# Moving part of an encoder layer's transfers from SyncE's queue to GpSimd's

## The chip, the cores and the metric

The kernel runs on one core of one Trainium2 chip. The metric is the device time of one execution in microseconds, lower is better; a time given for a kernel is the median of its runs. The core has TensorE (PE; weight loads are shown as PEld), VectorE (DVE), ScalarE (ACT), GpSimd (POOL) and SyncE (SP). Transfers are issued from an engine's queue: here SP's and, after the change, POOL's too. Each engine executes its own instructions in a fixed order, and an instruction that waits holds up those behind it.

## The reference

One layer of an encoder over 256 tokens of width 2048, in fp32:

```python
mod = silu(c) @ W_ada + b_ada            # 2048 x 12288: shift1, scale1, gate1, shift2, scale2, gate2
h = x * (1 + scale1) + shift1
x = layer_norm(alpha * x + gate1 * mixer(h))
h = x * (1 + scale2) + shift2
x = layer_norm(alpha * x + gate2 * peer(h))
```

mixer: one input projection (2048 x 11328), a bidirectional state-space scan with 32 heads in 2 chunks of 128 tokens (its decay rows are cumulative sums over time), a gated short convolution, group norms, and one output projection (4096 x 2048). peer: queries (2048 x 4096), two sets of 128 keys for each of 8 heads, the best 16 pairs, and gelu(h . u) times the gate times v over 16384 experts. All 16384 are computed here as dense products with expert_u and expert_v, with gates that are zero for those not chosen.

## The kernel before

**Weight tiles.** Nearly everything is a stream of weight tiles of 128 x 1024 fp32 (512 KB; w_inA's are 128 x 768). `wsplit` (L68 to L83) loads a tile into `raw`, lets ScalarE round it to fp32r (`hi`, L78) and VectorE subtract (`lo`, L81), and TensorE multiplies with both parts (`mm3`). `raw`, `hi` and `lo` have three buffers each. So SP may issue the next weight load when VectorE has finished `lo` of the tile three back.

**adaLN.** The six parts of `mod` are products of one vector with a 2048 x 2048 matrix each. They are made on VectorE: `ada_half` (L148 to L153) multiplies a 128 x 1024 tile of w_ada with the broadcast vector `scb` and sums along the row (L152). Parts 0 and 1 come in the front, 64 such tiles, loaded by `ada_load` (L281) into four buffers of 1 MB; parts 2, 3 and 4 beside the input and output projections, 96 tiles through two buffers `adaw` (`ada_step`, L163); part 5, 32 tiles, at the start of the expert_v stage through two quarters of the tile `big` (also L163). Those quarters take the last columns of expert_v later (L893).

**Stages, in order.** The front (w_inA, w_inB and the first adaLN parts: TensorE can use a row block d of h only when its two mod values are there); the rest of w_in beside the scan, which loads decay rows `bct` from DRAM (L529), written once as `acs_d` (L501); the output projection with `ax`, rows of x (L642); layer norm; the query projection with the keys `sk` (L710) and the residual written to `ax_d` (L692); expert_u, where the first 64 Gelu rows go to DRAM (`gel_d`, L841, from one buffer `ge`) and come back in the second half (`gb`, L849, two buffers); expert_v with part 5 of adaLN, whose result is written as `g2_d` in 4-byte pieces and read back broadcast as `g2b` (L914, L915); the last layer norm.

**What sets the order.** The program is written for a scheduler: it emits each engine's instructions in an order of its own, by the priorities given in the code (`high_priority(offset=...)`) and by its own estimate of when operands are ready. All 1245 transfers go out on SP's queue, in one such order.

## Time and profile before

| | |
|---|---|
| time, median of 3 runs | 2547.92 us (2544.36 to 2559.14) |
| profiled execution | 2552.61 us, of which the span is 2550.7 |
| TensorE busy | 2424.6 us (95%) |
| VectorE busy | 1862.2 us (73%) |
| ScalarE busy | 1381.3 us (54%) |
| GpSimd busy | 0.9 us |
| moved | 575.67 MB, mean 226 GB/s |
| granted TensorE clock, mean | 0.984 |

The busy time of an engine is the time in which one of its instructions executes; instructions that issue transfers are not counted. The shares are means over stages with different limits.

### The profile page before, as it was taken

Reading aid. Unit: us, or ns where it says so; the run is one execution under the profiler, and the core shown is the slowest. Engines: PE = TensorE matmul, PEld = TensorE weight load, DVE = VectorE, ACT = ScalarE, POOL = GpSimd, SP = SyncE. Lnnn points to the kernel's source line nnn. Section 1 sums busy time; section 2 is a strip of 40 time slices with the busy share of each in tenths; the row PEclk is TensorE's granted clock in tenths of the full one; section 3 lists DMA queues with packets and bytes.
Section 4 is the critical chain, followed back from the end, with each engine's and each line's share of the span. In section 5 each row is a group of like instructions: output and inputs, shape, how many; then the busy total and the mean of one; then the engine's idle time right before and its main releaser. Section 6 shows DMA issues by size and latency. Waiting matters only on the chain.

```text
span 2550.7 us, 44290 instructions
## 1 busy us (share of the span) xinstructions
PE 2424.6 (95%) x17122; PEld 2248.3 (88%) x17122; DVE 1862.2 (73%) x3255; ACT 1381.3 (54%) x2506; POOL 0.9 (0%) x7
## 2 busy tenths in 40 slices
PE   5889999999999899999999999999998999999997
PEld 5889888888899799999999999999886888888886
DVE  8788888989887799898888855555675555645545
ACT  3435476656444554499999944444443444544442
POOL 0000000000000000000000000000000000000000
PEclk9999999999999899999999999999999999999999
DMA  9886766778887565355666666666788655655554
GB/s 356 313 297 236 260 217 224 235 260 280 267 291 259 196 206 181 116 181 193 199 195 200 198 218 219 218 217 219 257 307 274 217 194 190 223 192 193 193 190 149
DMA packets 183252, 575.67 MB, mean 226 GB/s; under 512 B 22209, under 2 KB 44929, under 8 KB 182657
## 3 DMA queue, kind: packets, MB, share of 16 engines
q1 hardware_dynamic: 183042, 572.85, 67.3%
q8 instruction: 134, 2.20, 0.3%
q14 instruction: 76, 0.62, 0.1%
HBM read 560.10 MB, written 12.66 MB: 225 GB/s over the span
## 4 chain that ended last, share of the span: by engine, by line
PE 67%; DMA 15%; DVE 12%; ACT 3%; issue 2%; SPq 1%; DVEq 0%; ACTq 0%
PE ps_u L91 9%; PE ps_u L92 9%; PE ps_u L93 9%; PE ps_v L879 8%; PE ps_v L881 8%; PE ps_v L878 8%; DVE lo L81 5%; DMA adaw<-in_w_ada_dram 4%; DMA raw<-in_w_in_dram 3%; DMA big<-in_w_ada_dram 2%; ACT hi L78 2%; DVE adaw L152 2%; DMA raw<-in_w_inA_dram 2%; PE ps_q L93 2%; PE ps_q L92 2%
## 5 line engine op out<-in xcount | busy, mean ns | idle before, releaser
L81 DVE TENSOR_TENSOR lo<-raw,hi 128x1024 fp32r<-128x1024 f32 (+1 forms) x804 | 972.1, 1212 | 506.8 <-ACT hi L78 504.7
L78 ACT ACTIVATE hi<-raw 128x1024 fp32r<-128x1024 f32 (+1 forms) x804 | 843.6, 1051 | 884.6 <-PE ps_v L879 302.1
L91 PE MATMUL ps_u<-h2h,hi 128*128 128x256 f32 x2048 | 568.7, 278 | 0.0
L92 PE MATMUL ps_u<-h2l,hi 128*128 128x256 f32 x2048 | 568.1, 277 | 0.0
L93 PE MATMUL ps_u<-h2h,lo 128*128 128x256 f32 x2048 | 568.1, 277 | 0.0
L878 PE MATMUL ps_v<-hi,ah 128*128 128x512 f32 x992 | 390.1, 393 | 9.9 <-ACT hi L78 8.1
L879 PE MATMUL ps_v<-hi,al 128*128 128x512 f32 x992 | 390.7, 394 | 1.2 <-DVE al L120 1.2
L91 PEld LDWEIGHTS ps_u<-h2h,hi 128*128 128x128 f32 x2048 | 386.2, 189 | 0.0
L92 PEld LDWEIGHTS ps_u<-h2l,hi 128*128 128x128 f32 x2048 | 384.6, 188 | 0.0
L93 PEld LDWEIGHTS ps_u<-h2h,lo 128*128 128x128 f32 x2048 | 384.5, 188 | 0.0
L881 PE MATMUL ps_v<-lo,ah 128*128 128x512 f32 x992 | 268.9, 393 | 0.8 <-DVE lo L81 0.8
L878 PEld LDWEIGHTS ps_v<-hi,ah 128*128 128x128 f32 x992 | 187.5, 189 | 52.3 <-ACT hi L78 8.9
L879 PEld LDWEIGHTS ps_v<-hi,al 128*128 128x128 f32 x992 | 187.7, 189 | 43.0 <-DVE al L120 1.6
L91 PE MATMUL ps_in<-h2h,hi 128*128 128x256 f32 x768 | 222.3, 289 | 3.0 <-DVE mod L159 2.2
L881 PEld LDWEIGHTS ps_v<-lo,ah 128*128 128x128 f32 x992 | 186.8, 189 | 42.0 <-DVE lo L81 2.0
L93 PE MATMUL ps_in<-h2h,lo 128*128 128x256 f32 x768 | 217.6, 283 | 2.3 <-DVE lo L81 2.3
L152 DVE SCALAR_TENSOR_TENSOR adaw<-adaw,scb 128x1024 f32<-128x1024 f32 x160 | 193.1, 1219 | 35.3 <-DMA adaw<-in_w_ada_dram 35.0
L92 PE MATMUL ps_in<-h2l,hi 128*128 128x256 f32 x768 | 217.6, 283 | 0.0
L809 ACT ACTIVATE o<-eq,gT 128x128 fp32r<-128x128 f32 x512 | 161.4, 388 | 0.0
L91 PEld LDWEIGHTS ps_in<-h2h,hi 128*128 128x128 f32 x768 | 146.6, 191 | 9.0 <-issue 4.2
L93 PEld LDWEIGHTS ps_in<-h2h,lo 128*128 128x128 f32 x768 | 147.1, 191 | 4.6 <-DVE lo L81 2.9
L93 PE MATMUL ps_o<-y,lo 128*128 128x256 f32 x512 | 145.6, 284 | 5.0 <-DVE lo L81 4.9
(285 smaller groups left out, 3975.0 us busy)
## 6 DMA issues: line engine op xcount, KB each, us to landing
raw<-in_expert_u_dram SPq DMA_DIRECT2D x256, 512.0 KB, 4.5
raw<-in_expert_v_dram SPq DMA_DIRECT2D x248, 512.0 KB, 3.9
adaw<-in_w_ada_dram SPq DMA_DIRECT2D x160, 512.0 KB, 6.0
raw<-in_w_in_dram SPq DMA_DIRECT2D x110, 512.0 KB, 5.0
raw<-in_w_out_dram SPq DMA_DIRECT2D x64, 512.0 KB, 4.3
raw<-in_w_query_dram SPq DMA_DIRECT2D x64, 512.0 KB, 3.9
raw<-in_w_inB_dram SPq DMA_DIRECT2D x44, 512.0 KB, 4.4
big<-in_w_ada_dram SPq DMA_DIRECT2D x32, 512.0 KB, 5.6
```

Of the source, the lines that this page charges most:

```text
L78: A.activation(hi, raw, AF.Copy)
L81: V.tensor_tensor(lo, raw, hi.bitcast(F32), op=ALU.subtract)
L91: T.matmul(ps, wh, mh, start=start, stop=False)
L92: T.matmul(ps, wh, ml, start=False, stop=False)
L93: T.matmul(ps, wl, mh, start=False, stop=stop)
L152: V.scalar_tensor_tensor(w, w, 0.5, scb[:, cs], op0=ALU.mult, op1=ALU.mult, accum_out=macc[:, half, part % 2, d:d + 1])
L809: A.activation(o2[:, k], eq[:, i, 1].bitcast(F32), AF.Copy, scale=gT[:, k, t0 + i:t0 + i + 1])
L878: T.matmul(banks[tb][c], ah[:, ts], vh, start=start, stop=False)
L879: T.matmul(banks[tb][c], al[:, ts], vh, start=False, stop=False)
L881: T.matmul(banks[tb][c], ah[:, ts], vl, start=False, stop=stop)
```

## The change

`aside` is GpSimd's `dma_start`. It takes the place of SyncE's for adaLN's weights (but for the first step's in the front), the later blocks of x, the decay rows and their write, the residual's write, the keys, the staged Gelu rows both ways, and the vectors that are written and read back for the last stage. Weight tiles, the first inputs, the residual's reads, the last columns and the output stay on SyncE. No computation, buffer or priority is changed.

```diff
+    aside = nc.gpsimd.dma_start
...
     def ada_step(scb, ws, part, d):
         for half, w in enumerate(ws):
-            nc.sync.dma_start(w, I["w_ada"][part, d, :, half * 1024:(half + 1) * 1024])
+            aside(w, I["w_ada"][part, d, :, half * 1024:(half + 1) * 1024])
...
-                nc.sync.dma_start(wa[d, part][:, cs], I["w_ada"][part, d, :, cs])
+                (aside if d else nc.sync.dma_start)(wa[d, part][:, cs], I["w_ada"][part, d, :, cs])
...
-            nc.sync.dma_start(xt4[d // 4], I["xT"][:, d:d + 4])
+            aside(xt4[d // 4], I["xT"][:, d:d + 4])
...
-        nc.sync.dma_start(acs_d, acr.rearrange("h c t -> h (c t)"))
+        aside(acs_d, acr.rearrange("h c t -> h (c t)"))
...
-                nc.sync.dma_start(bct[:, dr].rearrange("p e c t -> p e (c t)"), bass.AP(
+                aside(bct[:, dr].rearrange("p e c t -> p e (c t)"), bass.AP(
...
-        nc.sync.dma_start(ax, I["xT"][:, d])
+        aside(ax, I["xT"][:, d])
...
-            nc.sync.dma_start(ax_d[:, :, d * P:(d + 1) * P].rearrange("b t d -> t b d"),
+            aside(ax_d[:, :, d * P:(d + 1) * P].rearrange("b t d -> t b d"),
...
-    nc.sync.dma_start(sk, I["sub_keys"])
+    aside(sk, I["sub_keys"])
...
-                nc.sync.dma_start(gel_d[e2], act_chunk(e2, wk, 1, step))
+                aside(gel_d[e2], act_chunk(e2, wk, 1, step))
...
-                nc.sync.dma_start(gb, gel_d[k])
+                aside(gb, gel_d[k])
...
-                nc.sync.dma_start(g2_d.rearrange("d p -> p d"), mod[:, 5])
-                nc.sync.dma_start(g2b, bass.AP(tensor=g2_d.tensor, offset=g2_d.offset, ap=[[0, P], [1, D]]))
+                aside(g2_d.rearrange("d p -> p d"), mod[:, 5])
+                aside(g2b, bass.AP(tensor=g2_d.tensor, offset=g2_d.offset, ap=[[0, P], [1, D]]))
```

The scheduler's order changes with it. Lines of the changed kernel are two higher than those of before from here on.

**The front.** SP's queue before, at its start, from the write of `sc_d` on (`adaw_189` and `adaw_192` are the two tiles of adaLN's second step, `raw` is a weight tile):

```order
L296 DMA sc_d<-scb 1x2048
L281 DMA adaw_189<-in_w_ada_dram 128x1024 x2
L281 DMA adaw_192<-in_w_ada_dram 128x1024 x2
L75 DMA raw<-in_w_inA_dram 128x768 x2
L281 DMA adaw_252<-in_w_ada_dram 128x1024 x2
L281 DMA adaw_255<-in_w_ada_dram 128x1024 x2
L75 DMA raw<-in_w_inA_dram 128x768 x2
L281 DMA adaw_315<-in_w_ada_dram 128x1024 x2
```

SP's queue of the changed kernel from the same row on:

```order
L298 DMA sc_d<-scb 1x2048
L77 DMA raw<-in_w_inA_dram 128x768 x9
L77 DMA raw<-in_w_inB_dram 128x1024
L77 DMA raw<-in_w_inA_dram 128x768
L77 DMA raw<-in_w_inB_dram 128x1024 x2
L77 DMA raw<-in_w_inA_dram 128x768
```

POOL's queue of the changed kernel, from its last fill on:

```order
L337 IOTA jp 128x128
L283 DMA adaw_189<-in_w_ada_dram 128x1024 x2
L283 DMA adaw_192<-in_w_ada_dram 128x1024 x2
L283 DMA adaw_252<-in_w_ada_dram 128x1024 x2
L283 DMA adaw_255<-in_w_ada_dram 128x1024 x2
L283 DMA adaw_315<-in_w_ada_dram 128x1024 x2
```

On SP the adaLN loads between the weight loads are gone, so that nine w_inA loads stand one behind the other; the same adaLN loads are the first transfers on POOL, in the order that they had.

**The output projection.** VectorE's order before, some way into the output projection (`adaw` is adaLN's multiplication, `lo` the split of a weight tile, `ln_a` and `ln_q` sums for the layer norm, `mod` the sums of adaLN):

```order
L152 SCALAR_TENSOR_TENSOR adaw,macc<-adaw,scb 128x1024
L192 TENSOR_TENSOR ln_a<-ln_a,rT 128x256
L197 TENSOR_TENSOR ln_q<-ln_q,ln_sq 128x256
L81 TENSOR_TENSOR lo<-raw,hi 128x1024
L158 TENSOR_TENSOR mod<-macc 128x1
L159 TENSOR_TENSOR mod<-mod,badaT 128x1
L81 TENSOR_TENSOR lo<-raw,hi 128x1024
L152 SCALAR_TENSOR_TENSOR adaw,macc<-adaw,scb 128x1024
L81 TENSOR_TENSOR lo<-raw,hi 128x1024
L152 SCALAR_TENSOR_TENSOR adaw,macc<-adaw,scb 128x1024
```

VectorE's order of the changed kernel at the same place:

```order
L160 TENSOR_TENSOR mod<-macc 128x1
L154 SCALAR_TENSOR_TENSOR adaw,macc<-adaw,scb 128x1024
L83 TENSOR_TENSOR lo<-raw,hi 128x1024
L194 TENSOR_TENSOR ln_a<-ln_a,rT 128x256
L199 TENSOR_TENSOR ln_q<-ln_q,ln_sq 128x256
L161 TENSOR_TENSOR mod<-mod,badaT 128x1
L154 SCALAR_TENSOR_TENSOR adaw,macc<-adaw,scb 128x1024
L83 TENSOR_TENSOR lo<-raw,hi 128x1024
L160 TENSOR_TENSOR mod<-macc 128x1
L154 SCALAR_TENSOR_TENSOR adaw,macc<-adaw,scb 128x1024
```

There is now a multiplication for each split. From the first tile of w_out on, the remaining multiplications stand among 20 splits or so, where before they were spread over 44.

**The expert_v stage.** VectorE's order before, in the middle of adaLN's last part (`big` is the multiplication, `al` a split of the activations):

```order
L152 SCALAR_TENSOR_TENSOR big_23146,macc<-big_23146 128x1024
L81 TENSOR_TENSOR lo<-raw,hi 128x1024
L152 SCALAR_TENSOR_TENSOR big_23146,macc<-big_23146 128x1024
L81 TENSOR_TENSOR lo<-raw,hi 128x1024 x2
L120 TENSOR_TENSOR al<-GA_12817,ah 128x512
L152 SCALAR_TENSOR_TENSOR big_23146,macc<-big_23146 128x1024
L81 TENSOR_TENSOR lo<-raw,hi 128x1024
L152 SCALAR_TENSOR_TENSOR big_23146,macc<-big_23146 128x1024
L81 TENSOR_TENSOR lo<-raw,hi 128x1024 x2
```

VectorE's order of the changed kernel at the same place:

```order
L154 SCALAR_TENSOR_TENSOR big_23146,macc<-big_23146 128x1024
L83 TENSOR_TENSOR lo<-raw,hi 128x1024
L154 SCALAR_TENSOR_TENSOR big_23146,macc<-big_23146 128x1024
L83 TENSOR_TENSOR lo<-raw,hi 128x1024
L154 SCALAR_TENSOR_TENSOR big_23146,macc<-big_23146 128x1024
L83 TENSOR_TENSOR lo<-raw,hi 128x1024
L122 TENSOR_TENSOR al<-GA_12817,ah 128x512
L154 SCALAR_TENSOR_TENSOR big_23146,macc<-big_23146 128x1024
L83 TENSOR_TENSOR lo<-raw,hi 128x1024
```

Two splits in a row no longer occur between multiplications: from the first of the 32 to the last there are 31 splits, where there were 43. The first load of the last columns on SP now follows the 37th weight tile of the stage.

## Rows read from the trace of the kernel before

**Rows 1.** The page of the profile: the span, and each engine's busy time.

```profile
span 2550.7 us, 44290 instructions
...
PE 2424.6 (95%) x17122; PEld 2248.3 (88%) x17122; DVE 1862.2 (73%) x3255; ACT 1381.3 (54%) x2506; POOL 0.9 (0%) x7
```

**Rows 2.** Busy us: length, PE, PEld, DVE, ACT, POOL, clock, DMA share, GB/s.

```profile
8.00:182.00 174.00, 139.53 (x1068) 133.86 (x1068) 142.50 (x247) 66.99 (x103) 0.00 (x0) 0.96 0.89 330
...
1825.00:1952.00 127.00, 126.22 (x549) 102.73 (x548) 95.23 (x118) 52.40 (x55) 0.00 (x0) 1.00 0.89 308
1955.00:1975.00 20.00, 11.92 (x45) 9.11 (x44) 6.26 (x6) 4.75 (x5) 0.00 (x0) 0.84 0.64 187
2000.00:2050.00 50.00, 50.00 (x220) 41.00 (x220) 25.10 (x24) 21.25 (x23) 0.00 (x0) 1.00 0.57 190
```

**Rows 3.** Waits between 50 and 212 us: who for whom, us, times, longest.

```profile
ACT hi L78 <- DMA raw<-in_w_inB_dram: 35.3, 22, 3.6
ACT hi L78 <- DMA raw<-in_w_inA_dram: 31.3, 8, 5.8
```

**Rows 4.** DMA issues, 50:212 and 2000:2400 us: count, KB each, median us to landing.

```profile
raw<-in_w_inA_dram SPq DMA_DIRECT2D x22, 384.0 KB, 7.1
...
raw<-in_expert_v_dram SPq DMA_DIRECT2D x146, 512.0 KB, 3.5
```

**Rows 5.** The split lo (L81) alone, in two stretches of the output projection.

```profile
651.00:796.00 145.00, 53.83 (x45) 0.98 0.87 290
800.00:846.00 46.00, 20.73 (x17) 1.00 0.67 213
```

**Rows 6.** Tile big, 1790 to 2060 us: adaLN's multiplication, its waits, loads' landing.

```profile
L152 DVE SCALAR_TENSOR_TENSOR big<-big x32: 1217/1225/1227, 1825.9 to 1951.6; 128x1024 f32<-128x1024 f32 x32
...
  DMA big<-in_w_ada_dram: 28.3, 29
...
DMA to landing us min/median/max: 4.3/5.6/14.6
```

**Rows 7.** The chain that ended last, 1870 to 1900 us: start, length, what.

```profile
1879.58 6.54 DMA big<-in_w_ada_dram
...
1888.54 0.33 SPq L75
...
1888.92 6.28 DMA big<-in_w_ada_dram
```

**Rows 8.** The first stretch with full DMA queues, columns as in rows 2.

```profile
20.00:30.00 10.00, 8.75 (x48) 8.29 (x49) 8.82 (x19) 4.82 (x8) 0.00 (x0) 1.00 1.03 409
```

**Rows 9.** DMA issues of the whole program, columns as in rows 4.

```profile
bct<-acs_d SPq DMA_DIRECT2D x32, 256.0 KB, 5.4
gel_d<-ge SPq DMA_DIRECT2D x64, 128.0 KB, 3.9
...
sk<-in_sub_keys_dram SPq DMA_DIRECT2D x1, 2048.0 KB, 13.0
...
ax<-ax_d SPq DMA_DIRECT2D x8, 256.0 KB, 3.0
```

**Rows 10.** The chain that ended last, 1950 to 1985 us.

```profile
1954.90 3.68 SPq L893
...
1958.68 12.12 DMA raw<-in_expert_v_dram
```

**Rows 11.** Instructions in order of time, 1300 to 1312 us, ScalarE, then SP.

```profile
1300.70 0.37 ACT L138 ACTIVATE ge<-ps_u 128x256 f32<-128x256 f32 x1
...
1304.13 0.39 ACT L818 ACTIVATE GA<-ps_g 128x124 f32<-128x124 f32 x1 [0.35 <-DVE GA L819]
...
1306.73 0.36 ACT L138 ACTIVATE ge<-ps_u 128x256 f32<-128x256 f32 x1
...
1301.45 0.33 SPq L841 DMA_DIRECT2D gel_d<-ge  x1
```

**Rows 12.** Who waited for the decay rows' load (L529), whole program.

```profile
  ACT Emat L536: 20.1, 13
```

More of the change, by code (lines that the diff above doesn't have):

```diff
@@ L861, in layer_kernel @@
         scb5 = big[:, 2:].rearrange("p a c -> p (a c)")
-        nc.sync.dma_start(scb5, bass.AP(tensor=sc_d.tensor, offset=sc_d.offset, ap=[[0, P], [1, D]]))
+        aside(scb5, bass.AP(tensor=sc_d.tensor, offset=sc_d.offset, ap=[[0, P], [1, D]]))
         banks = [[pv.tile([P, 512], F32, name="ps_v", tag="pm") for _ in range(4)] for _ in range(2)]
```

## The prediction

> **What bounds the kernel now.** I read the page first, then the busy time by stretches, then the waits and the chain in the stretches where TensorE is not full. TensorE is busy 95% of a span of 2550.7 us [rows 1], so about 126 us could be gained at most by moving transfers, and the question is where those lie. In the plain expert_v stretch TensorE is full and does 220 matmuls in 50 us; one weight tile of 1024 columns feeds 12 of them, so it eats a tile in 2.73 us [rows 2]. It is not full in three places that the change touches: the front (139.5 of 174 us), the output projection while adaLN steps run beside it, and the first 150 us of expert_v, which end in a hole of 8.1 us between 1955 and 1975 us [rows 2].
>
> In the front ScalarE's first half of each split (hi) waits for the weight tiles themselves, 31.3 and 35.3 us between 50 and 212 us [rows 3]. There a w_inA tile lands 7.1 us after its issue, where an undisturbed tile takes 3.5 us in the median [rows 4]: the adaLN tiles issued ahead of it on SP's queue, 2 MB per step, are in its way.
>
> Beside the output projection the same kind of tile needs longer too. From 651 to 796 us 45 splits (lo) pass in 145 us, which is 3.22 us each; from 800 to 846 us, with no adaLN step left, 17 pass in 46 us, 2.71 us each [rows 5]. In expert_v 32 adaLN steps run from 1825.9 to 1951.6 us, and VectorE waits for their loads 29 times, 28.3 us in all [rows 6]. The chain shows the loop: a load issued at 1879.58 lands 6.54 us later, VectorE multiplies (1.23 us) and splits the next weight tile, only then SP issues a weight load, and behind that the next adaLN load into the same buffer [rows 7]. Two buffers, 31 steps in 125.7 us: the loop is 8.1 us around. Its landing is 5.6 us in the median [rows 6], so 2.5 us of it are multiplication, the split and SP's turn.
>
> **The change part by part.** No work is added on TensorE, VectorE or ScalarE. 388 transfers leave SP's queue for POOL's, an engine that is busy 0.9 us of the span [rows 1], and this changes two things: who waits behind whom, and the order that the scheduler writes down for VectorE.
>
> *Front.* SP's order is now weight tiles alone; the adaLN steps load from POOL as their buffers come free. By 182 us 57 MB have moved (174 us at 330 GB/s), and the queue moves 409 GB/s when it is full [rows 2, 8]; so the bytes need 140 us. VectorE was busy 142.5 us there [rows 2], and the new order puts about 5 more adaLN multiplications of 1.22 us into the same number of splits: 149 us. That is the floor; the stretch as it is, 174 us, is the ceiling. Since VectorE takes turns in a fixed order and will wait for one stream or the other, I take the middle, 161: **13 us less**, between 25 and 0.
>
> *Output projection and expert_v.* Here the order matters. The written order now has the 32 multiplications of expert_v among 31 splits, one for one, where before there were 43 splits, and the last 20 in the output projection among some 21 splits of the 45. VectorE executes in order: a multiplication whose load is not there holds up the split behind it, and that holds up TensorE as soon as its three finished tiles are used. So a tile costs half a loop, R/2, as long as adaLN steps last, and 2.73 or 2.71 us after that. For expert_v: 31 x R/2 + 12 x 2.73 against 126 us; for the output projection 20 x R/2 + 24 x 2.71 against 145 us. Together 25.5 R + 98 - 271.
>
> What is R with POOL issuing? The multiplication stays, 1.23 us. The wait for the split and SP's turn goes; an issue is left, which I put at SP's 0.4 us. The landing is at best that of an undisturbed tile, 3.5 us [rows 4], and at worst today's 5.6 us [rows 6]; I take 4.6, because the load no longer stands behind a weight tile on one queue but still shares the engines with it. What POOL adds to a transfer no row shows, since POOL issues none before. Below, nothing. Above, I use the dearest difference that rows of equal size show for the handling of a transfer: 256 KB land in 5.4 us as small pieces (bct) and in 3.0 us as long rows (ax from ax_d), 2.4 us [rows 9]. adaLN's rows are 4 KB long, nearer to the lower end: 1.0 us. So R = 1.23 + 0.4 + 4.6 + 1.0 = 7.2 us, and the two stages come to 183.6 + 98 - 271 = **+10.6 us**: expert_v 18.3 slower, the output projection 8 faster. Bounds: R cannot pay below twice TensorE's pace, 5.46; above it is 1.63 + 5.6 + 2.4 = 9.6 us.
>
> The Trainium skill, "DMA: Bandwidth & Descriptors", section Latency and other measured facts, gives about 1 us to the first byte for a transfer issued from GpSimd and 0.6 us from SyncE; an estimate by that page would add 0.4 us in place of my 1.0, R would be 6.6, and the two stages would cost 15 us less than I say. No run so far shows it.
>
> *The hole at 1955.* SP issues g_d (8 KB in 4-byte pieces), then a load of the last columns that occupies it for 3.68 us, and the weight tile issued at 1958.68 lands 12.12 us later [rows 10]; g2b, which reads what g_d writes, comes next in SP's order. Both go to POOL, and nothing needs g2b before the end. **8 us less**; if the 4-byte pieces hold up the engines all the same, some 4.
>
> *Start of the query projection.* sk, 2 MB, lands in 13.0 us [rows 9], and some of the first weight tiles stand behind it on SP. **2 us less.**
>
> *At nothing, with a threshold.* gel_d, the write of each staged Gelu row, lands in 3.9 us on SP [rows 9], and there is one buffer: the next Gelu may not start before. One Gelu starts at 1300.70, its write is issued at 1301.45 and lands about 1305.35; the next Gelu starts at 1306.73 [rows 11]. So 1.4 us later costs nothing; with 1.0 us for POOL it is covered, by my upper value of 2.4 it is not: ScalarE would stand still 1.0 us, 64 times, with the next hi behind it, and what ScalarE idles there now (0.35 us per half) gives back some 0.4: 38 us. gb has two buffers and nothing waits for it.
>
> The decay rows (bct) stay behind adaLN loads on their queue as before; ScalarE waits 20.1 us for them now, 13 times [rows 12]. A microsecond more each costs 13 us if nothing covers it; I count nothing, as VectorE is the busier engine there. SP has no wait any more except for weight buffers, and for the first last-column load (L893 before), which stands after 37 expert_v tiles and waits until the adaLN buffers are done: the same time that the 31 splits take.
>
> Sum: -13 + 10.6 - 8 - 2 = **-12.4 us**. The profiled execution took 2552.6 us and 1.9 of them lie outside the span; 2540.2. It is 4.7 us above the median of the three runs, 2547.9; on that footing **2535 us**.
>
> **The rivals.** *Slower: the loop does not get shorter, and the order now asks for more of it.* If the two queues only share the same engines, the landing stays 5.6 us and the front stays as it is: R = 1.63 + 5.6 + 1.0 = 8.2, 25.5 x 8.2 + 98 - 271 - 8 - 2 = +26 us, 2574 by the median; at R = 9.6 it is +62, 2610, before the 38 us of a late gel_d. For it: the engines are already 0.89 busy in the front and in expert_v [rows 2]. Against: they move 409 GB/s elsewhere. The sum changes sign at R = 7.7 us with my front, at 7.2 with none. The Trainium skill, same page, section Issuing engines are not separate DMA queues, says that transfers from any engine run on the same engines and interleave, so that a second issuer saves issue time alone; by that rule this rival is what happens. Its chance, with that of a late gel_d, I put at 0.29.
>
> *It cancels.* R between 7.4 and 8.0: the front's gain is given back in expert_v; -7 to +8 us, about 2548. Chance 0.16.
>
> *Much faster.* POOL's loads land like undisturbed ones: R = 6.2 or less, front at its floor: 25.5 x 6.2 + 98 - 271 - 8 - 2 - 25 = -50 us, 2498. For it: nothing stands in front of the load any more. Against: both streams at TensorE's pace would need 1.05 MB per 2.73 us, 385 GB/s, close to the 409 of the fullest stretch. Chance 0.20.
>
> **How the numbers follow.** The forecast has 0.35. Half a per cent, 12.7 us, is about what a measurement of this kernel can tell from no change (three runs span 14.8 us). The forecast lies at that mark: 0.20 of it I count as faster, 0.15 as no change. Faster: 0.20 + 0.20 = 0.40; same 0.15 + 0.16 = 0.31; slower 0.29. The range leaves out the far end of the fast and of the slow case, a tenth each: 2500 to 2583. The likeliest case by itself spans 2523 to 2548.
>
> **What would show it.** Front: the waits of hi for w_inA and w_inB fall well below 66 us, w_inA lands in about 4 us, and the splits that take until 182 us are through by about 170. Expert_v: the 32 multiplications take about 112 us with 31 splits in them, TensorE is visibly short in that stretch, and the rest runs at 2.73 us a tile; the hole after g_d is gone. adaLN loads from POOL land in about 5.6 us, POOL's share included. The prediction is wrong if a landing is over 7 us (then expert_v alone eats all gains), or if Gelu waits for gel_d, or if ScalarE's waits for bct grow beyond 30 us, or if the front stays at some 174 us for 51 splits although w_inA lands early: then VectorE's order, not the transfers, was what held it.

## The result, and the profile after

The changed kernel is slower: 2619.3 us (median of 4 runs, 2601.0 to 2626.1) beside 2550.3 us before, ratio 1.0256, 95% interval 1.0208 to 1.0304. 2535 us was forecast. The profiled execution took 2624.2 us.

The page after, the span, the engines and the two queues (q1 carries what SyncE issues, q0 what GpSimd issues), to be read beside [rows 1]:

```profile
span 2622.5 us, 44540 instructions
PE 2450.6 (93%) x17122; PEld 2266.7 (86%) x17122; DVE 1857.1 (71%) x3255; ACT 1387.4 (53%) x2510; POOL 212.1 (8%) x395
...
q1 hardware_dynamic: 123266, 439.06, 51.3%
q0 software_dynamic: 38256, 133.79, 15.4%
```

VectorE has the same work, TensorE is busy 26 us longer, and 134 MB go by the other queue. GpSimd's 212 us are its 388 issues. Of TensorE's 26 us, 13.4 lie in expert_u (below) and 6.7 beside the scan, where its mean granted clock is 0.96 instead of 0.98. Busy time there, before, then after (columns as in [rows 2]):

```profile
212.60:651.50 438.90, 410.56 (x3075) 381.35 (x3073) 389.05 (x752) 276.62 (x571) 0.00 (x0) 0.98 0.73 244
```

```profile
221.00:684.30 463.30, 417.24 (x3066) 389.35 (x3066) 395.42 (x768) 281.84 (x578) 53.98 (x101) 0.96 0.71 236
```

**Where the time went.** All kernels round the same 804 weight tiles on ScalarE (hi). The start of the n-th hi (counted from 0) in one trace minus that in the trace before is the lag there, and the difference of two lags is what a stage lost. Tile 62 lies near the end of the front, w_out begins with 172, 260 lies behind the projections among the queries' weights, 420 near the middle of expert_u, expert_v begins with 556, and by 620 adaLN's last part and the hole are over (not so in the kernels that spread adaLN's last part). Before, these tiles start at 212.6, 929.2, 1437.0, 1810.1 and 2003.2 us. The table has every kernel of this study; the ratio is to the kernel before on the same chip. One of e3's four executions took 9324.55 us; its ratio leaves it out, the median given for it does not.

| kernel | ratio, 95% | front | to 260 | to 420 | to 556 | to 620 | rest |
|---|---|---|---|---|---|---|---|
| after | 1.0256 (1.0208, 1.0304) | +8.4 | +31.2 | -1.3 | +13.4 | +19.6 | +0.4 |
| after_again | one run, 2624.9 us | +5.5 | +33.9 | -0.7 | +13.4 | +20.0 | +0.3 |
| e1_ada | 1.0242 (1.0210, 1.0275) | +8.4 | +24.8 | 0 | 0 | +16.9 | +0.1 |
| e2_rest | 1.0120 (1.0068, 1.0171) | -5.6 | +25.1 | +1.2 | 0 | -0.1 | +0.2 |
| e3_spread | 1.0150 (1.0112, 1.0188) | +6.8 | +32.1 | +0.2 | 0 | -14.5 | +10.0 |
| e5_pin | 1.0293 (1.0259, 1.0328) | +13.5 | +54.4 | -0.8 | +13.4 | +2.3 | +0.5 |
| f1_queues | 1.0225 (1.0192, 1.0258) | +25.0 | +25.8 | +1.3 | +13.4 | +1.3 | +0.4 |
| f2_order | 1.0311 (1.0277, 1.0346) | +21.8 | +36.8 | +1.0 | 0 | +17.3 | +0.4 |
| g1_rows | 1.0183 (1.0153, 1.0212) | +24.3 | +12.7 | +1.5 | 0 | -2.6 | +0.1 |
| g2_steps | 1.0070 (1.0049, 1.0090) | -2.4 | +19.8 | +0.2 | 0 | +1.3 | +0.2 |
| g3_half | 1.0169 (1.0143, 1.0196) | -3.8 | +37.9 | -1.4 | 0 | +15.8 | +0.3 |
| g5_half_before | 0.9990 (0.9969, 1.0012) | -3.0 | -3.4 | +0.4 | 0 | +0.9 | +10.2 |
| h1_gb_sync | 1.0269 (1.0226, 1.0312) | +6.2 | +31.3 | -1.1 | +13.4 | +16.7 | +0.6 |
| h2_gb_gpsimd | 0.9994 (0.9973, 1.0016) | 0 | -6.4 | +0.9 | +13.4 | +2.4 | +0.2 |
| h3_again | one run, 2584.3 us | +10.4 | +26.4 | -0.6 | 0 | -12.9 | +8.6 |
| i1_start | 1.0290 (1.0257, 1.0322) | +8.2 | +31.0 | +0.1 | +13.4 | +17.2 | +0.2 |
| f3_pieces | 0.9974 (0.9946, 1.0002) | -1.0 | -6.3 | +0.6 | 0 | -12.3 | +6.0 |
| g4_best | 0.9972 (0.9947, 0.9996) | +1.0 | +1.1 | +0.1 | 0 | -12.1 | +3.0 |
| i2_best | 0.9966 (0.9941, 0.9991) | +1.0 | -5.3 | +0.5 | +13.4 | -12.7 | +4.5 |

h2, f3, g4 and i2 run the program of before up to expert_u or expert_v; in the projections they stand between -6.4 and +1.1, so a few microseconds there are the scatter of one execution.

Three things are visible at once: a lasting loss in the projections, 20 us in expert_v, and 13.4 us in the second half of expert_u, where nothing was foreseen. Most of the projections' loss lies beside the scan: 23.7 of the 31.2 us by tile 173.

**Front.** The waits between 50 and 212 us after, answering to [rows 3]:

```profile
ACT hi L80 <- DMA raw<-in_w_inB_dram: 52.3, 22, 5.9
...
ACT hi L80 <- DMA raw<-in_w_inA_dram: 29.2, 16, 5.5
```

DMA issues in the same stretch, after, then the one of before that [rows 4] lacks (count, KB, median us to landing):

```profile
adaw<-in_w_ada_dram POOLq DMA_DIRECT2D x46, 512.0 KB, 7.2
raw<-in_w_inB_dram SPq DMA_DIRECT2D x31, 512.0 KB, 6.6
raw<-in_w_inA_dram SPq DMA_DIRECT2D x21, 384.0 KB, 6.1
```

```profile
raw<-in_w_inB_dram SPq DMA_DIRECT2D x32, 512.0 KB, 4.6
```

w_inA lands a microsecond sooner, with only weight tiles ahead of it in its queue, but w_inB 2 us later, and these are 31 beside 21. Together ScalarE waits 81.5 us for weight tiles instead of 66.6.

**Expert_v.** adaLN's multiplications there, after, beside [rows 6]:

```profile
L154 DVE SCALAR_TENSOR_TENSOR big<-big x32: 1216/1225/1227, 1880.0 to 1989.9; 128x1024 f32<-128x1024 f32 x32
...
  DMA big<-in_w_ada_dram: 35.4, 24
...
DMA to landing us min/median/max: 3.3/5.3/16.0
```

109.9 us for 31 rounds, which is 7.1 us around two buffers: 7.2 was predicted, 112 us for the stretch.

**The hole.** The issue of g_d after, and the piece of the chain that crosses the hole (start, length, what), beside [rows 10]:

```profile
g_d<-mod POOLq DMA_DIRECT2D x1, 8.0 KB, 13.9
```

```profile
1993.71 15.10 DMA raw<-in_expert_v_dram
```

g_d is issued on GpSimd's queue at 1992.82, and a weight tile issued on SyncE's 0.9 us later lands 15.10 us after its issue. The hole has not moved with the queue.

**What went as predicted.** Other DMA issues after, beside [rows 9], and Gelu's whole wait for gel_d:

```profile
bct<-acs_d POOLq DMA_DIRECT2D x32, 256.0 KB, 5.6
gel_d<-ge POOLq DMA_DIRECT2D x64, 128.0 KB, 4.0
...
sk<-in_sub_keys_dram POOLq DMA_DIRECT2D x1, 2048.0 KB, 9.0
```

```profile
  DMA gel_d<-ge: 1.1, 3
```

### The profile page after: what moved, and what is told of

Read it like the earlier page. It is cut to its first block, busy times and chain, and to the rows that moved or that the text cites. A ratio compares the mean times of both kernels' runs of the same rounds, so it can differ in the third digit from the quotient of the medians.

```text
span 2622.5 us, 44540 instructions
## 1 busy us (share of the span) xinstructions
PE 2450.6 (93%) x17122; PEld 2266.7 (86%) x17122; DVE 1857.1 (71%) x3255; ACT 1387.4 (53%) x2510; POOL 212.1 (8%) x395
## 4 chain that ended last, share of the span: by engine, by line
PE 61%; issue 3%; DMA 3%; DVE 2%; ACT 1%; POOL 0%; DVEq 0%; POOLq 0%; ACTq 0%; SPq 0%
PE ps_u L94 9%; PE ps_u L93 9%; PE ps_u L95 9%; PE ps_v L880 8%; PE ps_v L883 7%; PE ps_v L881 7%; PE ps_q L94 2%; PE ps_q L93 2%; PE ps_q L95 2%; PE ps_o L95 1%; PE ps_o L93 1%; PE ps_o L94 1%; PE ps_g L816 1%; DMA big<-in_w_ada_dram 1%; DMA raw<-in_w_query_dram 1%
## 5 line engine op out<-in xcount | busy, mean ns | idle before, releaser
L880 PE MATMUL ps_v<-hi,ah 128*128 128x512 f32 x992 | 391.7, 395 | 10.2 <-ACT hi L80 8.3
L94 PEld LDWEIGHTS ps_in<-h2l,hi 128*128 128x128 f32 x768 | 150.6, 196 | 3.9 <-issue 3.1
```

The source lines that it names most:

```text
L94: T.matmul(ps, wh, ml, start=False, stop=False)
L880: T.matmul(banks[tb][c], ah[:, ts], vh, start=start, stop=False)
```

## The experiments

### Half of the change at a time

e1 puts only adaLN's weights (ada_step, ada_load, scb5) on GpSimd's queue, e2 all but these:

```diff
 e1_ada, against the changed kernel
-                aside(gel_d[e2], act_chunk(e2, wk, 1, step))
+                nc.sync.dma_start(gel_d[e2], act_chunk(e2, wk, 1, step))
...
 e2_rest, against the changed kernel
-            aside(w, I["w_ada"][part, d, :, half * 1024:(half + 1) * 1024])
+            nc.sync.dma_start(w, I["w_ada"][part, d, :, half * 1024:(half + 1) * 1024])
...
```

> adaLN's weights alone on GpSimd's queue, all else on SyncE's as before. Theory (the order): VectorE's new order, one adaLN multiplication for each split of a weight tile, is what costs in the projections and in expert_v; this kernel still has it, so expert_v's 32 multiplications still take about 110 us and the projections lose their 34 us; only the slower matmuls of expert_u's second half (427 instead of 443 in 50 us, 14 us) are gone if GpSimd's loads of the Gelu rows made them slow: about 2605 us. Rival (the shared GpSimd queue: adaLN loads held up behind decay rows and residual rows): those rows are off GpSimd's queue here, so the projections are as before: about 2575 us.

> All but adaLN's weights on GpSimd's queue; adaLN's weights back on SyncE's. VectorE's written order is the dense one of the changed kernel all the same (31 splits among the 32 multiplications of expert_v). Theory (the order): the loop of a load on SyncE was 8.1 us around, two buffers, so the 32 multiplications take some 31 x 8.1 / 2 = 126 us with 31 splits instead of 43, 33 us slower than before in expert_v, and the projections lose about as much as in the changed kernel: 2610 us or more. Rival (the queue): with adaLN on SyncE again, projections and expert_v are as before, and only expert_u's second half is slower: 2550 to 2565 us.

Measured: 2612.5 us and 2577.8 us. e1 keeps 24.8 us of the projections' loss and 16.9 of expert_v's without decay rows or residual rows on GpSimd: the rival falls. e2's expectation rested on an order that the kernel does not have: its trace shows 43 splits among expert_v's 32 multiplications, as before, and expert_v then loses nothing. But 25.1 us are lost in the projections, with adaLN's loads on SyncE and its multiplications on average one split from their old places, so adaLN's order alone cannot be the cause there.

### The order against the queue

e3 ties each adaLN step of expert_v behind the split at which the program names it; e5 ties each adaLN multiplication behind the split of the same number as before (`last_lo[0]` is the latest split of a weight tile, `los` all splits so far, `AFTER_LO` before's numbers):

```diff
 e3_spread
-                ada_step(scb5, raw5[:2], 5, e2 // 6)
+                with tc.issue_after(last_lo[0]):
+                    ada_step(scb5, raw5[:2], 5, e2 // 6)
 e5_pin
+        n = next(AFTER_LO)
+        with tc.issue_after(los[n - 1]) if 0 < n <= len(los) else nullcontext():
             V.scalar_tensor_tensor(w, w, 0.5, scb[:, cs], op0=ALU.mult, op1=ALU.mult,
```

> The changed kernel, but each adaLN step of expert_v is tied behind the split of the weight tile at which the program names it: two multiplications for each 12 splits instead of one for each. Theory (the order): no wait for an adaLN load is left in expert_v, a tile takes 2.73 us all along, 31 x 2.73 = 85 us in place of 110: 25 us less than the changed kernel, about 2594 us. Rival (the queues share the engines and every adaLN load delays weight tiles): the 16 MB still pass, and expert_v gains less than 8 us: 2611 us or more.

> The changed kernel with its queues as they are, but every adaLN multiplication tied behind the same numbered split of a weight tile as before the change (43 splits among the 32 multiplications of expert_v). Theory (the order): the projections get back most of their 34 us, the 32 multiplications of expert_v take 43 x 2.73 = 118 to 126 us with 43 splits, 20 us gained; what stays is 6 us at the start and 14 us in expert_u: about 2570 us. Rival (the queue): the waits stay with the queue, and the time is within 10 us of the changed kernel's 2619 us.

2591.8 us and 2631.2 us. In expert_v both do what the order theory says: spread steps turn a loss of 19.6 us into a gain of 14.5, and before's spacing leaves 2.3 of it. But e3 gives 10.0 us back in the rest, 7.1 of them between tiles 748 and 766, where g_d is now written and loads beside it land late (from the chain of e3):

```profile
2384.89 13.27 DMA big<-in_expert_v_dram
```

In the projections e5 loses 54.4 us, more than the change: pinning one kind of instruction let all others be ordered anew around it. So the next pair fixes the whole order of VectorE, ScalarE and TensorE, in both directions (the order of the transfers within a queue stays the scheduler's):

```diff
         layer_kernel(tc, args, out)
+        pin(tc, nc)
...
+            if last is not None:
+                tc.add_manual_dep(own[at], last.name, edge(), reason="pin")
+            last = own[at]
```

`pin` walks through a table and ties each instruction of an engine behind its predecessor there. f1 is the changed kernel with before's table, f2 the kernel before with the changed kernel's.

> The queues of the changed kernel, but VectorE, ScalarE and TensorE execute all their instructions in exactly the order that they had before the change (a table fixes it). Theory (the order): the written order of the compute engines is the cause; here it is the old one, so expert_v is as before (126 us for its first 43 splits) and the projections lose at most the 13 us of later decay rows; with 6 us at the start about 2565 us. Rival (the queue): transfers on GpSimd's queue are the cause whatever the order, the projections lose 30 us or more again: 2600 us or more.

> All transfers on SyncE's queue as before the change, but VectorE, ScalarE and TensorE execute in exactly the order of the changed kernel. Theory (the order): the loss comes without GpSimd: a loop of 8.1 us around for two multiplications, so expert_v's 31 splits take 31 x 4.05 us + 12 x 2.73 us = 158 us where it was 126, and the projections lose some 30 us: about 2610 us. Rival (the queue): on the old queue the new order costs little, within 10 us of before: 2540 to 2562 us.

2613.6 us and 2632.0 us: neither theory holds for the whole. By stages the four cases (order, queue) are:

| lost, us | new order, old queue | old order, new queues | both |
|---|---|---|---|
| front | 21.8 | 25.0 | 8.4 |
| projections | 36.8 | 25.8 | 31.2 |
| expert_v | 17.3 | 1.3 | 19.6 |

In expert_v it is the order: the queues alone cost 1.3 us. The same multiplications in f2, all on SyncE's queue, then in f1, on GpSimd's in the old order:

```profile
L152 DVE SCALAR_TENSOR_TENSOR big<-big x32: 1216/1225/1227, 1886.1 to 1996.2; 128x1024 f32<-128x1024 f32 x32
...
DMA to landing us min/median/max: 3.2/5.4/15.3
```

```profile
L154 DVE SCALAR_TENSOR_TENSOR big<-big x32: 1214/1220/1226, 1893.0 to 2018.7; 128x1024 f32<-128x1024 f32 x32
...
DMA to landing us min/median/max: 4.1/6.2/14.0
```

In the new order the 31 rounds take 110.1 us on SyncE and 109.9 on GpSimd: the loop is 7.1 us on either. In the old order they take 125.7 us on either. A load lands as early from GpSimd as from SyncE in the new order (5.3 and 5.4 us), and 0.6 us later in the old one (6.2 and 5.6).

In the front each order fits its own queues, and crossing them costs 22 to 25 us. In the projections either half alone costs about as much as both; why the two do not add is open.

What the new order does there shows in who waits for VectorE. Some waits of ScalarE and TensorE in the projections, before, then in f2:

```profile
PE ps_y L558 <- DVE Emat L551: 11.6, 10, 2.6
...
ACT y L119 <- DVE cv L441: 8.6, 7, 2.9
...
ACT t L138 <- DVE t L424: 5.1, 4, 2.0
```

```profile
PE ps_y L558 <- DVE Emat L551: 20.0, 9, 5.8
ACT y L119 <- DVE cv L441: 19.5, 8, 10.1
ACT t L138 <- DVE t L424: 17.5, 5, 7.3
```

25.3 us before, 57.0 in f2. In f2 the scan's steps on VectorE have about ten more adaLN multiplications ahead of them than before, nine of them from the scan's start, and as many splits. That the waits come from these is not shown.

### What the queue costs in the projections and in the front

Both kernels have before's whole order. g1 moves only adaLN's later steps of the front, blocks of x and the decay rows with their write to GpSimd; g2 only ada_step and scb5:

```diff
 g1_rows, against f1
-            aside(w, I["w_ada"][part, d, :, half * 1024:(half + 1) * 1024])
+            nc.sync.dma_start(w, I["w_ada"][part, d, :, half * 1024:(half + 1) * 1024])
...
 g2_steps, against f1
-                aside(bct[:, dr].rearrange("p e c t -> p e (c t)"), bass.AP(
+                nc.sync.dma_start(bct[:, dr].rearrange("p e c t -> p e (c t)"), bass.AP(
...
```

> The compute engines in the order of before (fixed by a table). On GpSimd's queue only adaLN's later steps of the front, the later blocks of x, and the decay rows with their write; all else on SyncE's. Theory (each decay row costs more from GpSimd, with one buffer in the loop): the front loses what it lost with all moved transfers on GpSimd in this order, 27 to 30 us by split 62, and the projections another 13 us or so: about 2597 us. Rival (adaLN's steps on GpSimd hold up the projections, the decay rows don't): nothing more is lost after split 62, about 2583 us.

> The compute engines in the order of before (fixed by a table). On GpSimd's queue only adaLN's steps of the projections and of expert_v. The front is then that of before. Theory (of the 24 us that the projections lost with all moved transfers on GpSimd, half is due to the decay rows): 11 us here between splits 62 and 260, nothing in expert_v: about 2565 us. Rival (adaLN's steps are the cause): 24 us there, about 2578 us.

2597.0 us and 2571.7 us. In g1 the projections lose 12.7 us, the 13 that were expected for the decay rows, and the front 24.3. The expected reason did not come with the number: a decay row lands in 5.4 us, as in [rows 9], and ScalarE waits for them 4.5 us longer than in [rows 12]:

```profile
ACT Emat L538 <- DMA bct<-acs_d: 24.6, 14, 5.5
```

In g2 adaLN's steps cost 19.8 us, between the two expectations. DMA issues of the projections, before, then g2:

```profile
raw<-in_w_out_dram SPq DMA_DIRECT2D x64, 512.0 KB, 4.3
```

```profile
adaw<-in_w_ada_dram POOLq DMA_DIRECT2D x93, 512.0 KB, 5.9
raw<-in_w_out_dram SPq DMA_DIRECT2D x64, 512.0 KB, 5.3
```

The same stretch, the waits of hi for w_in and w_out, before and in g2:

```profile
ACT hi L78 <- DMA raw<-in_w_in_dram: 51.2, 27, 4.2
...
ACT hi L78 <- DMA raw<-in_w_out_dram: 18.8, 11, 2.9
```

```profile
ACT hi L80 <- DMA raw<-in_w_in_dram: 59.1, 30, 4.3
...
ACT hi L80 <- DMA raw<-in_w_out_dram: 39.9, 22, 3.5
```

With the adaLN loads on the other queue a w_out tile lands a microsecond later, and ScalarE waits 21 us longer for them. That is about what the stage lost, but it is not where it was lost: 16.4 of the 19.8 us are gone by tile 173, beside the scan, and 3.4 beside w_out. Beside the scan hi waits 7.9 us longer for w_in, and TensorE is busy 8.8 us longer with the same tiles, at a lower mean granted clock. The row of g2 for the stretch that the result shows for before:

```profile
210.20:665.50 455.30, 419.38 (x3085) 388.55 (x3083) 389.53 (x751) 276.40 (x571) 33.26 (x63) 0.96 0.69 234
```

Whether the lower clock comes of the waits, no run separates. For the front, f1 has the landings that belong to before's order on the new queues (50 to 237 us); w_inB takes 5.4 us for 4.6, w_inA 5.3 for 7.1:

```profile
raw<-in_w_inB_dram SPq DMA_DIRECT2D x32, 512.0 KB, 5.4
raw<-in_w_inA_dram SPq DMA_DIRECT2D x23, 384.0 KB, 5.3
```

g3 (the changed kernel) and g5 (before), each with its order fixed, take 16 MB out of the front:

```diff
         for part in range(2):
+            if d % 2:
+                wa[d, part] = wa[d - 1, part]
+                continue
             wa[d, part] = w0.tile([P, D], F32, name="adaw0", tag="adaw0")
```

> The changed kernel with its order fixed, but in the front each second adaLN step loads nothing and multiplies the tiles of the step before once more (so its values are not the reference's): 16 MB less in the front, with the same instructions on VectorE. Theory (both queues feed the same 16 engines, which are 0.9 to 1.0 busy there, and an adaLN load takes from the weight tiles what it no longer delays in the queue): w_inB lands in less than 5 us instead of 6.6, and split 51 comes at least 15 us earlier than in the changed kernel: about 2600 us. Rival (VectorE's order and work hold the front): split 51 comes within 5 us of the changed kernel's, about 2615 us.

> The kernel before with its order fixed, but in the front each second adaLN step loads nothing and multiplies the tiles of the step before once more (its values are not the reference's): 16 MB less in the front. Theory (the front is held by the bytes that pass through the shared engines, on one queue as on two): split 51 comes 8 us or more earlier than before, w_inA lands in about 5 us instead of 7.1: about 2542 us. Rival (VectorE's order and work hold the front of before): split 51 comes within 3 us of before's, about 2550 us.

2598.6 and 2555.3 us. DMA issues between 50 and 212 us, g3, then g5:

```profile
raw<-in_w_inB_dram SPq DMA_DIRECT2D x32, 512.0 KB, 5.0
```

```profile
raw<-in_w_inA_dram SPq DMA_DIRECT2D x22, 384.0 KB, 4.1
```

Tile 51 comes 10.9 us sooner in g3 than in the changed kernel (lag -7.1 instead of +3.8), and so do its neighbours: short of the theory's 15, outside the rival's 5. On two queues the bytes hold the front, though not they alone. In g5 tile 51 comes 6.7 us sooner than before, but it is an exception: tiles 50 and 52 come 0.9 and 2.0 sooner, tile 62 3.0, and h2, which runs before's program there, strays by up to 3.5. So on one queue the rival stands: w_inA lands in 4.1 us instead of 7.1, and the front is hardly shorter.

g5's gain is not in its time. In the profiled execution expert_v's rest loses 10.2 us, nearly all of it evenly, because the matmuls run at a slower pace with TensorE full and the granted clock at 1.00. Busy time from 2050 to 2100 us, before, then g5:

```profile
2050.00:2100.00 50.00, 50.00 (x220) 41.05 (x219) 25.07 (x23) 22.24 (x24) 0.00 (x0) 1.00 0.58 190
```

```profile
2050.00:2100.00 50.00, 50.00 (x216) 40.51 (x215) 24.67 (x24) 21.20 (x23) 0.00 (x0) 1.00 0.57 187
```

What sets that pace is as open as in expert_u below.

i1 loads adaLN's second step on SyncE behind the first inputs again:

```diff
-                (aside if d else nc.sync.dma_start)(wa[d, part][:, cs], I["w_ada"][part, d, :, cs])
+                (aside if d > 1 else nc.sync.dma_start)(wa[d, part][:, cs], I["w_ada"][part, d, :, cs])
```

> The changed kernel, but adaLN's second step in the front is loaded on SyncE, behind the first inputs, as before. Theory (its 2 MB, issued by GpSimd at 1.4 us, delay the first inputs on the shared engines): the tenth split comes within 1 us of before's instead of 6 us late, and 6 us of it reach the end: about 2613 us. Rival (the later steps on GpSimd cause it): still 5 to 6 us late at the tenth split, 2619 us.

2630.9 us; tile 10 still starts 5.5 us late. The theory falls. The instructions of i1 in order of time, SP, then POOL, show what is left: GpSimd's steps at 12.01 and 14.56 us are issued beside the first weight tiles. That these cost the 5.5 us is not shown.

```profile
10.38 3.45 SPq L283 DMA_DIRECT2D adaw<-in_w_ada_dram  x4
14.45 22.03 SPq L77 DMA_DIRECT2D raw<-in_w_inA_dram  x7
```

```profile
12.01 1.06 POOL L283 DMA_DIRECT2D adaw<-in_w_ada_dram  x2 [9.95 <-DVE adaw L154]
14.56 1.05 POOL L283 DMA_DIRECT2D adaw<-in_w_ada_dram  x2 [1.49 <-DVE mod L160]
```

### The pace of expert_u

> The changed kernel once more, for the pace of TensorE in the second half of expert_u. If the slow pace (427 matmuls in 50 us) belongs to the program with its GpSimd loads, it is 427 again. If it varies from execution to execution, 443 may be seen, and the time would then be about 2610 us.

> The changed kernel with the reads of the staged Gelu rows (gb) back on SyncE. Theory (those reads on GpSimd's queue are needed for the slow matmuls): 443 matmuls in 50 us in expert_u's second half, 13 us less, about 2606 us. Rival (the pace has nothing to do with that queue): 427 again, 2619 us.

> The kernel before with the reads of the staged Gelu rows (gb) alone on GpSimd's queue. Theory (those reads are enough to slow the matmuls, in some executions): 427 matmuls in 50 us in the profile, or times that scatter by some 13 us more than before's. Rival (other transfers on GpSimd are needed too): 443, and the time of before, 2552 us.

> The changed kernel with expert_v's adaLN steps spread, once more; its first profile had 443 matmuls in 50 us in expert_u's second half. Theory (the pace varies from execution to execution): 427 may be seen now, and the time is then about 2605 us instead of 2592. Rival (the program decides): 443 again, about 2592 us.

```diff
 h1_gb_sync (after)
-                aside(gb, gel_d[k])
+                nc.sync.dma_start(gb, gel_d[k])
 h2_gb_gpsimd (before)
-                nc.sync.dma_start(gb, gel_d[k])
+                nc.gpsimd.dma_start(gb, gel_d[k])
```

2624.9, 2623.8, 2554.3 and 2584.3 us. Busy time between 1600 and 1650 us (columns as in [rows 2]) before, after, in e2 (gb on GpSimd), in h1 (gb on SyncE) and in i2 (no transfer on GpSimd at all):

```profile
1600.00:1650.00 50.00, 50.00 (x443) 50.00 (x442) 29.04 (x39) 21.89 (x28) 0.00 (x0) 1.00 0.67 217
```

```profile
1600.00:1650.00 50.00, 50.00 (x427) 50.00 (x426) 28.01 (x36) 20.63 (x28) 4.34 (x9) 1.00 0.66 211
```

```profile
1600.00:1650.00 50.00, 50.00 (x443) 50.00 (x442) 28.37 (x37) 22.27 (x28) 5.37 (x10) 1.00 0.68 217
```

```profile
1600.00:1650.00 50.00, 50.00 (x427) 50.00 (x426) 27.76 (x36) 21.49 (x27) 0.00 (x0) 1.00 0.66 209
```

```profile
1600.00:1650.00 50.00, 50.00 (x427) 50.00 (x426) 28.11 (x36) 20.80 (x27) 0.00 (x0) 1.00 0.66 212
```

h1 and i2 end the theory that GpSimd's queue is needed. h2 loses the 13.4 us in its profile too and has the median of before. The two repeats came out as their first profiles did (427 and 443), though after and e3 have the same instructions up to that point. What sets the pace stays open; it is not the queue.

### Expert_v on one queue

f3 is the kernel before with spread steps, and the 128 results of each step written at once; g4 also ties the last columns' splits to their tiles; i2 also ties their loads:

```diff
 f3_pieces
+                with tc.issue_after(last_lo[0]):
+                    ada_step(scb5, raw5[:2], 5, e2 // 6)
+                    ada_sum(5, slice(e2 // 6, e2 // 6 + 1))
+                nc.sync.dma_start(g2_d[e2 // 6].rearrange("(p one) -> p one", one=1), mod[:, 5, e2 // 6:e2 // 6 + 1])
...
-                ada_sum(5, slice(0, ND))
-                nc.sync.dma_start(g2_d.rearrange("d p -> p d"), mod[:, 5])
 g4_best
+                with tc.issue_after(last_hi[0]), tc.issue_after(last_lo[0]):
+                    next(last, None)
 i2_best
+            with tc.issue_after(last_raw[0]):
+                nc.sync.dma_start(raw5[n % 4], I["expert_v"][NE - LAST + n // 2, n % 2])
```

> The kernel before, with each adaLN step of expert_v tied behind the split at which the program names it, and its 128 results written to DRAM at once after each step, 16 writes of 512 B in place of one of 8 KB, all on SyncE. Theory (the block of 2048 pieces of 4 bytes holds up the weight tiles behind it, on either queue): the 8 us hole is gone, and so are the 2 us of waits among the steps; about 2538 us. Rival (the hole comes from the other transfers around it, the first last-column load that occupies SyncE): the hole stays, moved behind the last step, 2546 us.

> The kernel before with adaLN's steps of expert_v spread and their results written in 16 pieces, all on SyncE, and now the splits of the last columns tied behind the weight tile at which the program names them. Theory (in the kernel without that tie ScalarE stood 19.6 us waiting for last columns, which put 8 to 12 us of lag back between splits 748 and 766): the 20 us gained by split 700 stay to the end: about 2533 us. Rival (that lag comes from the bytes of the last columns, 4 MB beside the weight tiles): it stays at 2544 us.

> The kernel before with expert_v's adaLN steps spread and written in 16 pieces, the splits of the last columns tied to their tiles, and their loads tied behind weight loads four pairs of tiles ahead; all on SyncE. Theory (the last columns' loads stood too early in SyncE's queue and held up weight loads behind them): the 18 us gained by split 700 stay to the end, about 2535 us. Rival (their bytes cost the time): 5 us are lost again between splits 700 and 780, about 2543 us.

2544.1, 2545.0 and 2548.4 us, ratios 0.9974, 0.9972 and 0.9966. All three gain 12 to 13 us by tile 620. Each of the 16 writes lands in 10.5 us in f3, and the slowest weight tiles beside them in 8 to 12, but the hole is gone: where the last write, g2b and the first last-column loads pass (2335 to 2375 us), TensorE is busy 38.33 of 40 us. All three lose 3 to 6 us again after tile 620, and neither tie removes that. The bytes of the last columns are what is left of the two explanations; no run shows them to be the cause. The intervals just reach or miss 1: a gain of 0.3%.

```profile
g_d<-mod SPq DMA_DIRECT2D x16, 0.5 KB, 10.5
```

```profile
2335.00:2375.00 40.00, 38.33 (x167) 30.82 (x166) 24.62 (x28) 20.23 (x22) 0.00 (x0) 1.00 0.80 272
```

## Why the prediction was wrong

Two steps failed above all: the sum held that an early landing of the weight tiles shortens the front, and it had no term for the scan.

- **The front, -13.** Measured +8.4. The failing sentence is that weight tiles alone on SyncE land early. w_inA landed 1.0 us sooner, w_inB 2.0 later, and 6.0 us were lost by tile 10. Of the two marks that the prediction set, w_inA at 4 us and hi's waits well below 66 us, neither came. And the landing was not what held the front of before: in g5 w_inA lands in 4.1 us, and the front is 3.0 us shorter. The prediction had named this too, as a sign of being wrong: VectorE's order, not the transfers.
- **The projections.** This is the largest miss: +31.2 against -8 for the adaLN loop there. The loop's formula was not bad: the 20 tiles beside the last adaLN steps took 78.2 us, 3.9 each where 3.6 was put, and the 23 tiles after them 2.74 us each where 2.71 was; tiles 173 to 216 lost 3.4 us. But 23.7 us were lost earlier, from tile 62 to 173, beside the scan, for which the sum had nothing. The prediction took the busy VectorE there as cover for later decay rows and asked for no other cost. The runs show two, each by itself: the new order on the old queue loses 34.9 us there (f2), the new queues in the old order 18.9 (f1; with adaLN's steps alone moved 16.4, g2). How they come to 23.7 together stays open. The 13 us named for decay rows without cover were met by luck (12.7 in g1): the landing was no microsecond later there.
- **Expert_v, +18.3.** Measured +19.6, with R = 7.1 for 7.2. The size and the mechanism (one multiplication for each split) were right. The terms of R were not: 4.6 us were put for a landing freed of the old queue and 1.0 for GpSimd, where 5.3 came on GpSimd's queue and, in the same order, 5.4 on SyncE's: there was nothing to win by leaving the queue and nothing to pay for GpSimd. The errors cancelled. f2 shows that R is the same on the old queue; the 8.1 us that the prediction read before belong to the old order, since f1 takes 125.7 us for the same 31 rounds on GpSimd's queue.
- **The hole, -8.** Measured 0. Its cause was read as SyncE's order, the load behind g_d. It goes with g_d itself, one write of 8 KB in 4-byte pieces: weight tiles from SyncE's queue wait beside it whichever queue it is on, late loads follow it to 2384 us in e3, and in 16 smaller writes it leaves no hole (f3). The prediction had named this case, but with 4 us of gain left.
- **gel_d and its threshold of 1.4 us, bct's landing.** Right: Gelu waits 1.1 us in all; 5.6 us.
- **sk, -2.** Not to be told from the scatter: the stage stands at -1.3, and between -1.4 (g3) and +1.3 (f1) in other kernels that have sk on GpSimd's queue.
- **expert_u.** 13.4 us of the profiled execution's 71.8 have no term, and by h1 and i2 none is owed to the queue.

The slower rival had the sign and part of the reason: two queues that share the engines are what f1 loses by in the front and the projections, but not what expert_v loses by. Its size, 26 to 62 us, holds the 58.4 that remain without expert_u's, but by another way: its R of 8.2 did not come, and its 0 in the front and nothing beside the scan were too kind. The Trainium skill, "DMA: Bandwidth & Descriptors", section Issuing engines are not separate DMA queues, has transfers from all engines run on the same DMA engines and interleave. The traces agree: in before's order w_inB's landing rose from 4.6 to 5.4 us in f1, and w_out's from 4.3 to 5.3 in g2, though w_inA's, with no adaLN load ahead of it, fell from 7.1 to 5.3. The Trainium skill, same page, section Latency and other measured facts, has 1 us to GpSimd's first byte against 0.6 us; the landings of 512 KB neither show nor exclude that, 0.1 us less from GpSimd in one order and 0.6 more in the other.

## What to carry to other kernels

Before transfers move to a second queue, ask what the scheduler will make of it: here the moved loads changed the order of VectorE, and in expert_v that alone was the loss. Nor did the second queue take one stream out of the other's way here: in before's order w_inA landed sooner (5.3 us for 7.1), but w_inB and w_out later (5.4 for 4.6, 5.3 for 4.3), and both stages lost. Ask too whether the landing holds the stage at all: g5 had w_inA 3.0 us sooner at each tile and the front only 3.0 us shorter in all. A wait that grows by as much as a stage loses need not be the loss; see where the lag arises, as in g2. To tell order from queue, fix the whole order of the compute engines and change one at a time; pinning only the suspected instructions moved all others.

## What the runs showed of the hardware

- Two profiled paces of the same matmuls with TensorE full and its granted clock at 1.00: 443 and 427 in 50 us over the second half of expert_u, 220 and 216 over the rest of expert_v (g5), with no transfer, order or queue that all slow kernels share.
- One write of 8 KB in 4-byte pieces on GpSimd's queue (g_d) goes with a 512 KB transfer on SyncE's that lands after 15.10 us; on SyncE's own queue with one of 12.12 us. In 16 portions among the weight tiles, on SyncE's queue, each lands in 10.5 us, and they cost nothing that shows by tile 620.
- An issue occupies GpSimd for 0.53 us (1.18 for g_d). Loads of 512 KB issued there land in 5.3 us where SyncE's take 5.4 (after and f2), and in 6.2 where SyncE's take 5.6 (f1 and before).
